# A four-layer decoder trunk on one core: out-projection parts as separate jobs, and two weight splits queued at other places

## The chip, the core and the metric

The kernel runs on one core of a Trainium2 chip. Five engines with queues of their own take part: TensorE (PE in the profile, with its weight loads shown apart as PEld), VectorE (DVE), ScalarE (ACT), GpSimd (POOL) and SyncE (SP), which issues the DMAs. Each engine runs its instructions in the order in which they were queued, and waits on semaphores for what other engines make. The metric is the device time of one launch in microseconds; the number given for a kernel is the median of several runs.

## What is computed

Four layers over 512 tokens of width 1024, in fp32. The mixers are, in turn, latent attention (MLA), sliding-window attention (SWA), forgetting attention (FoX), and MLA again. The part that all layers share:

```
for i in range(DEPTH):                    # 4 layers
    h = x @ w_in                          # q, k, v (or low-rank parts) and a gate
    o = attention(h)                      # 16 heads of 64
    y = (o * silu(gate)) @ w_out          # the out-projection, 1024 x 1024
    x = layernorm(ALPHA * x + y, ln_g[i], ln_b[i])
```

## The kernel before

**Products in split fp32.** Every operand of a product is held as a pair of fp32r tiles, hi (a cast) and lo (the rest), and a product is three matmuls: hi·hi, then the two mixed ones. In the out-projection and in other products with tokens on the output rows the order per contraction slab of 128 is hi·hi, lo·hi (the activation's lo), hi·lo (the weight's lo).

**Weights.** All weights lie in one packed array as units of up to 128x1024 values, in the order of use. `_raw` loads a unit into one of three raw buffers (`wr`) by an SP DMA. `_split(i)` brings all units up to i that are not yet split: ACT casts the raw tile to hi (L306) and POOL, or DVE for out-projection units, subtracts to get lo (L310, two instructions of up to 512 columns). Then the load of the unit two further on is issued. `W(key)` returns a unit and asks for the splits up to three units ahead, though not beyond `self.hold`. A unit of the next layer is not split before `finish` has raised `self.layer`.

**The order of instructions.** The kernel is traced as a program, and a scheduler in the compiler puts each engine's instructions in order by its own estimate of when each is ready. Inside `manual_schedule(engines={PE})` PE keeps the traced order instead, and inside `finish` DVE keeps it too. `run_heads` traces PE's work from the hand-written strings `ORDER[layer]`: each word is a letter and a count of matmuls. s is the next logits matmul, t the next transpose of probabilities, o the next matmul of probabilities and values. f, g and h take the next matmul of the first, second and third job in a list; a job that has come to its count at the front is dropped. The list holds the projections still to be made (gates, queries, keys) and, at its end, the out-projection, which before the change is one job of all its parts in a row: three token blocks of the left half (`half` 0) with contraction slabs 0 to 5, then their slab 6, then the right half and the left half's fourth block with slabs 0 to 6. f, g and h all mean that last job once nothing stands before it.

**The pair outputs.** After the two heads of a pair, ACT and DVE evacuate the result (L543, L544), POOL multiplies by the gate (L551), ACT casts to oT hi (L552) and POOL makes oT lo (L325). Slab p of the out-projection reads oT of pair p. The names A, B, C below are the left-half blocks 0, 1, 2; the number is the slab, and a, b, c are its three matmuls: A5a reads oT hi of pair 5 (heads 10 and 11), A5b reads oT lo, A5c reads hi again.

**The seam of two layers.** `tail` makes the last two heads with what is left of the out-projection (`st["order"]`) in between, and `finish` does the residual and LayerNorm by token block in the order of `FINISH[layer]`: r is the residual (L586), s the mean and squares (L612, ACT L614), t the variance (DVE L619) and 1/std (POOL power, L620), a and b the two halves of the apply (DVE L634, two instructions each, b needs 1/std), x the eight transposes to x^T on PE (L389) with ACT's cast (L393) and DVE's rest (L325). Block 0's x^T is what the next layer's first matmuls read. In the same stretch POOL splits the next layer's first units.

**The start.** Before layer 0, four blocks of x are transposed (`x_transposes`), and the first weight units are loaded and split when the first layer asks for them.

Of the kernel before, what the change touches and what calls it, by code (L numbers as in the profile page):

```python
# [16 lines left out]
ALU = mybir.AluOpType  # L17
# [6 lines left out]
DEPTH = 4  # L24
# [176 lines left out]
class Net:  # L201
# [178 lines left out]
    def x_transposes(self, xt, tb, banks=None):  # L380

        nc = self.nc
        for g in range(2):
            pool, tag = banks or (self.ps_t, "pt")
            ps = pool.tile([128, 512], F32, tag=tag, name=self.nm("pxt"))
            for k in range(4):
                c = (4 * g + k) * 128
                v = ps[:, k * 128:(k + 1) * 128]
                nc.tensor.transpose(v, xt[:, c:c + 128], self.ident[:])  # L389
            src = ps[:].rearrange("p (k n) -> p k n", n=128)  # L390
            hi = self.xT[:, 0, 4 * g:4 * g + 4, tb * 128:(tb + 1) * 128]
            lo = self.xT[:, 1, 4 * g:4 * g + 4, tb * 128:(tb + 1) * 128]
            nc.scalar.copy(hi, src)  # L393
            self.lo(lo, src, hi)

    def xh(self, k):
# [160 lines left out]
    def out_part(self, layer, st):  # L557

        st["acc"] = {}
        st["done"] = 0  # L560
        st["stat"] = self.p_st.tile([128, NT, 4], F32, tag="stat", name=self.nm("stat"))
        self.load_residual(layer, st)
        parts = [(0, tb, range(6)) for tb in range(3)] + [(0, tb, [6]) for tb in range(3)]
        parts += [(half, tb, range(7)) for half, tb in ((1, 0), (1, 1), (1, 2), (0, 3))]
        for half, tb, ks in parts:
            for _ in self.out_mm(layer, st, half, tb, list(ks), False):
                st["done"] += 1 if self.fine else 3
                yield

    def out_mm(self, layer, st, half, tb, ks, stop):  # L570
        if (half, tb) not in st["acc"]:
            if (half, tb) in ((1, 0), (1, 1)):
                st["acc"][(half, tb)] = self.ps_s.tile([128, 512], F32, tag="ss", name=self.nm("po"))
            elif (half, tb) in ((1, 2), (0, 3)):
                st["acc"][(half, tb)] = self.ps_t.tile([128, 512], F32, tag="pt", name=self.nm("po"))
            else:
                st["acc"][(half, tb)] = self.bank()
        out = st["acc"][(half, tb)][:]
        oT = st["oT"]
        return self.tokproj_steps(out, lambda k: (self.W(layer, "O", half, k // 2), (k % 2) * 512), 512,  # L580
                                  lambda k, a, b: oT[k // 2][:, k % 2, a, b * 128:(b + 1) * 128], tb, ks, ks[0] == 0, stop, 3)
# [34 lines left out]
    def ln_rstd(self, st, tb):  # L616
        nc = self.nc
        s = st["stat"][:, tb, 3:4]
        nc.vector.tensor_scalar(s, s, 1.0 / D, LN_EPS, op0=ALU.mult, op1=ALU.add)  # L619
        nc.gpsimd.tensor_tensor(s, s, self.half[:, 0:1], op=ALU.pow)  # L620

    def ln_apply(self, layer, st, tb, part):
        nc = self.nc
# [30 lines left out]
    def run_heads(self, layer, st, make, pre=None, npre=0):  # L654

        kind = layer % 3
        st["P"], st["PT"], st["oT"] = {}, {}, []
        st["np"] = 3 if kind == 0 else 2
        self.heads = 0

        def size(n):
            return {"K": 6, "Q": 9, "R": 9}.get(n, 24) if kind == 0 else 96 if n == "V" else 24

        def logits():
            for h in range(H - 1):
                if h == 13 and kind == 0:
                    self.cq_done(layer)
                for i, f in enumerate(st["s_fn"](h, st)):
                    for j, _ in enumerate(f()):
                        if i == NT - 1 and j == st["np"] - 1:  # L670
                            self.head_done()
                        yield

        jobs = [[npre, pre]] if npre else []
        jobs += [[size(n), make[n](a)] for n, a in STREAM[kind]]
        st["order"] = self.out_part(layer, st)
        jobs.append([1000, st["order"]])
        runs = {"s": logits(), "t": chain.from_iterable(f() for h in range(H - 2) for f in st["t_fn"](h, st)),
                "o": chain.from_iterable(self.attn_pv(h, st) for h in range(H - 2))}
        self.fine = True  # L680
        with self.tc.manual_schedule(engines={mybir.EngineType.PE}):
            for w in ORDER[layer].split():
                for _ in range(int(w[1:])):
                    job = jobs[min("fgh".index(w[0]), len(jobs) - 1)] if w[0] in "fgh" else [0, runs[w[0]]]
                    next(job[1])
                    job[0] -= 1
                    while jobs[0][0] == 0:
                        jobs.pop(0)
            assert len(jobs) == 1 and all(next(r, None) is None for r in runs.values())
            self.tail(layer, st)  # L690

    def tail(self, layer, st):
# [12 lines left out]
    def finish(self, layer, st):  # L705
        nc = self.nc
        self.load_gb(layer, st)
        self.layer = layer + 1
        if layer < DEPTH - 1:
            self.new_xT()  # L710

        def mm(half, tb, ks=(7,)):
            self.run(self.out_mm(layer, st, half, tb, list(ks), True))

        def res(tb, half):
            self.out_res(layer, st, half, tb, st["acc"][(half, tb)][:])

        S0, S1 = lambda tb: self.ln_stats(st, tb), lambda tb: self.ln_rstd(st, tb)
        A = lambda tb, i: self.ln_apply(layer, st, tb, i)

        def X(tb):
            self.x_transposes(st["r"][tb], tb, (self.ps_s, "ss") if tb % 2 == 0 else (self.ps_t, "pt"))

        def ends(tb):
            assert st["done"] >= (84, 105, 126, 147)[tb]
            mm(0, tb)
            if tb < 3:
                mm(1, tb)

        last_mm = self.out_mm(layer, st, 1, 3, list(range(8)), True)  # L730
        todo = {"f": lambda n: self.run(islice(st["order"], n)), "k": ends, "m": lambda n: self.run(islice(last_mm, n)),
                "r": lambda t: (res(t, 0), res(t, 1)), "h": lambda t: res(t, 0), "i": lambda t: res(t, 1), "s": S0, "t": S1,
                "a": lambda t: A(t, 0), "b": lambda t: A(t, 1), "z": lambda t: self.ln_apply_side(st, t), "x": X}
        with self.tc.manual_schedule(engines={mybir.EngineType.DVE}):
            for w in FINISH[layer].split():
                todo[w[0]](int(w[1:]))

    def cq_done(self, layer):
        self.cq_free = layer + 1
# [351 lines left out]
@with_exitstack  # L1091
def trunk(ctx, tc, t):
    net = Net(ctx, tc, t)
    nc = net.nc
    x0 = []
    for tb in range(NT):
        r = net.p_kk.tile([128, D], F32, tag="kk", name=net.nm("x0"))
        for c in range(0, D, 512 if tb == 0 else D):
            w = 512 if tb == 0 else D
            nc.sync.dma_start(r[:, c:c + w], t["x"][tb * 128:(tb + 1) * 128, c:c + w])  # L1100
        x0.append(r)
        if tb < 2:
            net._raw(1 + tb)
    net.new_xT()
    net.warm_up()
    for tb in range(NT):
        net.x_transposes(x0[tb], tb)
    for layer in range(DEPTH):
        (net.mla, net.swa, net.fox)[layer % 3](layer)

# [30 lines left out]
```

## Time and profile before

| what | value |
|---|---|
| runs, median (lowest to highest) | 1026.9 us (1026.78 to 1029.99), 3 runs |
| the profiled execution's own time | 1026.01 us |
| its span in the profile | 1024.2 us |
| instructions | 16213 |
| mean TensorE clock granted | 0.986 of full |
| DVE, ACT, POOL busy | 598.3, 620.8, 510.7 us |
| moved by DMA | 116.79 MB, 114 GB/s |

The profile is of one execution. The span runs from the first to the last instruction; the execution's own time is 1.8 us longer. A row of the timeline gives the start and the length in microseconds, the engine, the source line, the operation, the tile written, the tiles read, the shape and the count of instructions merged in the row; in brackets stands how long the engine was idle before the row, and what ended that idle time. `pp`, `po`, `ss`, `oo`, `ptt` and `pxt` are PSUM tiles (projections, out-projection, logits, head outputs, transposed probabilities, transposed x). In a row of several matmuls, the length is from the first start to the last end, and neighbouring rows can overlap since matmuls are pipelined. In tables by stretch, each engine has its busy time, and PEclk is the clock that TensorE was granted as a share of full.

### The profile page before, as it was taken

To read this page: it belongs to the slowest core of one execution; us is meant where nothing else is said; L and a number is where in the kernel's file an instruction comes from. 1 tells how busy PE (TensorE), PEld (TensorE's weight loads), DVE (VectorE), ACT (ScalarE), POOL (GpSimd) and SP (SyncE) were. 2 spreads that over 40 slices of the span, in tenths; PEclk is the share of its full clock that TensorE was granted. 3 is DMA by queue.
4 is the path that set the end of the run, shared out by engine and by line. 5 is a ranking of instruction groups with operands and counts; after the bars stand their busy time and mean duration, and the time that the engine had idled before them with its cause. 6 is when DMAs were issued, how large, how long until landed. Compare 5 with 4: busy or idle time off the path is not lost.

```text
span 1024.2 us, 16213 instructions
## 1 busy us (share of the span) xinstructions
PE 985.8 (96%) x5512; PEld 856.9 (84%) x5512; DVE 598.3 (58%) x1501; ACT 620.8 (61%) x1354; POOL 510.7 (50%) x572
## 2 busy tenths in 40 slices
PE   8999999999999999899999999997999999999995
PEld 7979888877988888688888888985779888888784
DVE  2467666935546667528325644664547466667827
ACT  4378888843357777523446766663533478888722
POOL 5746655335156663432556666543254647664213
PEclk9999999999999999899999999998999999999998
DMA  6353332634342213223434323353224354334322
GB/s 225 119 157 92 98 106 66 205 111 146 133 143 84 83 63 124 91 94 128 133 120 141 105 88 120 91 144 120 84 84 146 97 145 127 85 94 124 103 62 83
DMA packets 37795, 116.79 MB, mean 114 GB/s; under 512 B 5440, under 2 KB 5696, under 8 KB 37456
## 3 DMA queue, kind: packets, MB, share of 16 engines
q1 hardware_dynamic: 37712, 115.75, 36.5%
q8 instruction: 44, 0.72, 0.3%
q14 instruction: 39, 0.32, 0.1%
HBM read 92.62 MB, written 8.42 MB: 99 GB/s over the span
## 4 chain that ended last, share of the span: by engine, by line
PE 47%; DVE 3%; issue 2%; POOL 1%; ACT 1%; DMA 1%; DVEq 0%; POOLq 0%; SPq 0%; ACTq 0%
PE pp L322 31%; PE ss L322 4%; PE po L322 4%; PE oo L322 3%; PE ptt L514 3%; DMA wr<-in_w 1%; PE pxt L389 1%; POOL r L650 1%; DVE w L310 1%; DVE r L634 0%; POOL P L462 0%; DVE PT L325 0%; ACT P L451 0%; DVE wo L310 0%; DVE r L586 0%
## 5 line engine op out<-in xcount | busy, mean ns | idle before, releaser
L322 PE MATMUL pp<-xT,w 128*128 128x512 f32 (+1 forms) x1440 | 352.4, 387 | 0.0
L310 POOL TENSOR_TENSOR w<-wr,w 128x512 fp32r<-128x512 f32 (+1 forms) x202 | 242.2, 1224 | 193.0 <-ACT w L306 127.2
L322 PEld LDWEIGHTS pp<-xT,w 128*128 128x128 f32 x1440 | 256.1, 188 | 44.2
L462 POOL TENSOR_TENSOR P<-P,rs 128x256 f32<-128x256 f32 (+2 forms) x192 | 113.0, 616 | 136.8 <-DVE rs L457 131.3
L306 ACT CAST w<-wr 128x1024 fp32r<-128x1024 f32 (+5 forms) x121 | 116.1, 964 | 87.4 <-PE pp L322 43.5
L451 ACT ACTIVATE P<-P,m 128x256 f32<-128x256 f32 (+3 forms) x256 | 137.8, 539 | 45.9 <-DVE m L1069 17.0
L325 DVE TENSOR_TENSOR PT<-ptt,PT 128x384 fp32r<-128x384 f32 (+1 forms) x176 | 104.0, 600 | 52.6 <-ACT PT L500 51.3
L500 ACT CAST PT<-ptt 128x384 fp32r<-128x384 f32 (+1 forms) x176 | 88.3, 515 | 47.6 <-PE ptt L514 34.6
L322 PE MATMUL pp<-w,xT 128*128 128x256 f32 (+2 forms) x768 | 112.7, 300 | 2.9 <-ACT xT L393 2.5
L322 PEld LDWEIGHTS pp<-w,xT 128*128 128x128 f32 x768 | 105.8, 191 | 4.6 <-ACT xT L393 3.1
L322 PE MATMUL oo<-PT,v 128*128 128x256 f32 (+3 forms) x512 | 106.6, 313 | 2.3 <-DVE o L544 1.6
L322 PEld LDWEIGHTS oo<-PT,v 128*128 128x128 f32 x512 | 83.5, 189 | 14.0 <-DVE o L544 2.6
L322 PE MATMUL pp<-w,oT 128*128 128x512 f32 x288 | 82.5, 422 | 10.9 <-ACT oT L552 7.5
L322 PE MATMUL ss<-kt,q 128*128 128x128 f32 (+3 forms) x384 | 81.8, 328 | 2.2 <-ACT kt L838 1.6
L322 PE MATMUL pp<-cT,w 128*128 128x512 f32 x312 | 81.6, 397 | 0.0
L885 DVE CUSTOM_DVE_ANT_0 P<-ss,mask 128x128 f32<-128x128 f32 (+3 forms) x128 | 61.1, 484 | 32.4 <-PE ss L322 24.7
L514 PE MATMUL ptt<-ident,P 128*128 128x128 f32 x480 | 78.5, 275 | 1.5 <-DVE PT L325 0.8
L322 PEld LDWEIGHTS pp<-w,oT 128*128 128x128 f32 x288 | 56.0, 202 | 23.4 <-ACT oT L552 8.1
L322 PE MATMUL po<-wo,oT 128*128 128x512 f32 x288 | 71.5, 396 | 0.0
L322 PEld LDWEIGHTS ss<-kt,q 128*128 128x128 f32 x384 | 60.7, 189 | 8.8 <-ACT kt L838 2.2
L514 PEld LDWEIGHTS ptt<-ident,P 128*128 128x128 f32 x480 | 57.1, 140 | 11.8 <-PE ss L322 2.1
L544 DVE TENSOR_TENSOR o<-oo,o 64x512 f32<-64x512 f32 x64 | 43.9, 686 | 37.4 <-ACT o L543 36.7
(120 smaller groups left out, 1425.9 us busy)
## 6 DMA issues: line engine op xcount, KB each, us to landing
wr<-in_w SPq DMA_DIRECT2D x106, 512.0 KB, 3.5
q<-rq SPq DMA_DIRECT2D x64, 128.0 KB, 2.4
xd<-r SPq DMA_DIRECT2D x12, 512.0 KB, 2.9
r<-xd SPq DMA_DIRECT2D x12, 512.0 KB, 3.4
wr<-in_w SPq DMA_DIRECT2D x16, 336.0 KB, 3.4
kd<-kd SPq DMA_DIRECT2D x20, 256.0 KB, 3.2
tq<-in_cs SPq DMA_DIRECT2D x8, 512.0 KB, 4.0
cb<-cd SPq DMA_DIRECT2D x16, 256.0 KB, 3.9
```

Of the source, the lines that this page charges most:

```text
L306: nc.scalar.copy(w[0][:, :c], r[:, :c])
L310: eng.tensor_tensor(w[1][:, a:b], r[:, a:b], w[0][:, a:b].bitcast(F32), op=ALU.subtract)
L322: self.nc.tensor.matmul(out, l, r, start=start, stop=stop)
L325: (eng or self.nc.vector).tensor_tensor(out, src, hi.bitcast(F32), op=ALU.subtract)
L389: nc.tensor.transpose(v, xt[:, c:c + 128], self.ident[:])
L451: nc.scalar.activation(v, v, AF.Exp, bias=m[:, c:c + 1], scale=-1.0, accum_out=sums[:, c:c + 1])
L462: nc.gpsimd.tensor_tensor(v, v, rs[:, c:c + 1].to_broadcast([128, v.shape[1]]), op=ALU.mult)
L500: nc.scalar.copy(pt[:, 0, :n], ps[:, :n])
L514: nc.tensor.transpose(ps[:, c:c + 128], Ps[qb][:, kb * 128:(kb + 1) * 128], self.ident[:])
L544: nc.vector.tensor_tensor(o[a, :], o_ps[a, :], o[a, :], op=ALU.add)
L650: nc.gpsimd.tensor_tensor(v, v, st["gb"][2 * part + c][:], op=op)
L885: nc.vector.tensor_tensor_reduce(out=P[:, :n], in0=ps[:, :n], in1=self.mask[:, S - n:], scale=1.0, scalar=3e38, op0=ALU.add, op1=ALU.min, ...
```

## The change

There are three edits.

1. `out_part` returns a list of ten jobs, one for each part, where it was one generator. f, g and h are no longer cut off at the last job: g and h now reach the second and third part of the out-projection while an earlier part is unfinished. The `ORDER` strings are the same. The tail gets the chain of the jobs that are left.
2. In `finish`, `self.hold` is set so that the calls of `W` split two units of the next layer where they split three. The third is split after the `FINISH` steps have been traced, and inside `issue_after(st["pow"][1])`: its POOL instructions are queued behind block 1's 1/std, with no wait for it to end. ACT's cast of that unit has no such edge.
3. At the start, unit 0 is split inside `issue_after(net.cast)`, traced after block 0's transposes: ACT's cast of it is queued behind ACT's second x^T cast.

What edit 1 does to PE's order follows from the strings. In layer 0 nothing changes. In the others (the count of instructions in brackets):

```
layer 1 before: A0a..A4c  s14(2) A5a s14(2) A5b A5c  B0a..B3c  o12(3) t13(4) o12(5)
                B4a t13(3) B4b B4c B5a B5b B5c  C0a..C0c  o13(8)
layer 1 after:  A0a..A4c  s14(2) B0a s14(2) B0b..B4c  o12(3) t13(4) o12(5)
                A5a t13(3) B5a A5b A5c B5b B5c  C0a..C0c  o13(8)
layer 2 before: A4a..A5c  B0a..B3b o12(1) B3c s14(2) t12(3) o12(3) B4a B4b s14(2) B4c B5a..C0b
                t13(4) C0c C1a s14(2) C1b C1c C2a o12(1) C2b o12(3) C2c s14(2) t13(3) C3 t13(3) o13(8)
layer 2 after:  A4a..A4c  B0a..B4b o12(1) B4c s14(2) t12(3) o12(3) A5a B5a s14(2) C0a..C1c
                t13(4) C2a C2b s14(2) C2c A5b A5c o12(1) B5b o12(3) B5c s14(2) t13(3) C3 t13(3) o13(8)
layer 3 before: A5a A5b A5c B0a B0b o12(1) B0c s14(6) B1a..
layer 3 after:  A5a B0a B0b B0c B1a o12(1) A5b s14(6) A5c B1b..
```

The same matmuls are made in each; what is left for the tail is the same too. The third unit of edit 2 is the first key unit in layer 1 (128x1024), the third value unit in layer 2 (128x544) and the third unit of the low-rank projection in layer 3 (128x672).

```diff
@@ def x_transposes(self, xt, tb, banks=None):
-            nc.scalar.copy(hi, src)
+            self.cast = nc.scalar.copy(hi, src).ins
             self.lo(lo, src, hi)
@@ def out_part(self, layer, st):
         st["stat"] = self.p_st.tile([128, NT, 4], F32, tag="stat", name=self.nm("stat"))
-        self.load_residual(layer, st)
         parts = [(0, tb, range(6)) for tb in range(3)] + [(0, tb, [6]) for tb in range(3)]
         parts += [(half, tb, range(7)) for half, tb in ((1, 0), (1, 1), (1, 2), (0, 3))]
-        for half, tb, ks in parts:
+
+        def part(half, tb, ks):
+            if "r" not in st:
+                self.load_residual(layer, st)
             for _ in self.out_mm(layer, st, half, tb, list(ks), False):
                 st["done"] += 1 if self.fine else 3
                 yield
+
+        return [[3 * len(ks), part(half, tb, ks)] for half, tb, ks in parts]
@@ def ln_rstd(self, st, tb):
-        nc.gpsimd.tensor_tensor(s, s, self.half[:, 0:1], op=ALU.pow)
+        st["pow"][tb] = nc.gpsimd.tensor_tensor(s, s, self.half[:, 0:1], op=ALU.pow).ins
@@ def run_heads(self, layer, st, make, pre=None, npre=0):
-        st["order"] = self.out_part(layer, st)
-        jobs.append([1000, st["order"]])
+        jobs += self.out_part(layer, st)
...
-                    job = jobs[min("fgh".index(w[0]), len(jobs) - 1)] if w[0] in "fgh" else [0, runs[w[0]]]
+                    job = jobs["fgh".index(w[0])] if w[0] in "fgh" else [0, runs[w[0]]]
...
-            assert len(jobs) == 1 and all(next(r, None) is None for r in runs.values())
+            assert all(next(r, None) is None for r in runs.values())
+            st["order"] = chain.from_iterable(g for _, g in jobs)
             self.tail(layer, st)
@@ def finish(self, layer, st):
         self.layer = layer + 1
+        st["pow"] = {}
+        first = self.index[(layer, "O", 1, 3)] + 1
+        self.hold = first + 1
...
                 todo[w[0]](int(w[1:]))
+        self.hold = len(self.units)
+        if layer < DEPTH - 1:
+
+            with self.tc.issue_after(st["pow"][1]):
+                self._split(first + 2)
@@ def trunk(ctx, tc, t):
         net.x_transposes(x0[tb], tb)
+        if tb == 0:
+            with tc.issue_after(net.cast):
+                net._split(0)
```

## The prediction

> **What bounds the kernel now.** I read the page's first part, then the waits of TensorE. PE is busy for nearly the whole span, so time can come only from its idle gaps and from stretches in which it runs slowly.
>
> ```profile
> PE 985.8 (96%) x5512; PEld 856.9 (84%) x5512; DVE 598.3 (58%) x1501; ACT 620.8 (61%) x1354; POOL 510.7 (50%) x572
> ...
> PE pp L322 <- ACT oT L552: 7.5, 2, 3.9
> PE pxt L389 <- DVE r L634: 4.4, 5, 2.0
> PE pp L322 <- POOL oT L325: 3.2, 2, 2.6
> PE pp L322 <- ACT xT L393: 2.5, 1, 2.5
> ```
>
> The columns of a wait are its total, how often, and the longest. Three kinds matter, and each edit aims at one: 10.7 us for oT in front of an out-projection matmul (edit 1), 4.4 us for block 0's apply at the seams (edit 2), 2.5 us at the start (edit 3). The table by stretches of 5 us then says where PE was slow without being idle.
>
> ```profile
> 410.00:415.00 5.00, 1.40 (x6) 1.03 (x5) 4.41 (x8) 2.69 (x5) 2.92 (x4) 0.93 0.56 167
> 415.00:420.00 5.00, 4.87 (x13) 3.70 (x12) 1.00 (x5) 2.67 (x10) 1.56 (x3) 0.50 0.00 0
> ...
> 705.00:710.00 5.00, 2.12 (x4) 1.42 (x5) 0.00 (x0) 0.19 (x1) 3.62 (x4) 0.50 0.01 4
> 710.00:715.00 5.00, 5.00 (x14) 3.86 (x14) 0.00 (x0) 0.00 (x0) 0.00 (x0) 0.53 0.00 0
> ...
> 765.00:770.00 5.00, 4.64 (x17) 3.79 (x18) 5.00 (x8) 2.52 (x4) 5.00 (x5) 0.66 0.73 213
> ```
>
> The third column from the right is the granted clock. It drops to half behind the two oT stalls, and to 0.66 behind the longest seam wait. So a stall costs its idle time and some microseconds at half speed behind it. Meanwhile the other engines and the DMA have almost nothing to do: removing these stretches takes time from nobody.
>
> The Trainium skill, "TensorE: Matmul & The Clock Gate", Part 1, says that about 3.4 us without PE activity halve the clock, and the same time of activity restores it; the oT stalls of 3.6 us and more agree.
>
> **Edit 1, layer 1.** PE's timeline:
>
> ```profile
> 407.69 2.88 PE L322 MATMUL pp<-w,oT 128*128 128x512 f32 x12
> 410.42 0.40 PE L322 MATMUL ss<-kd,q 128*128 128x256 f32 x2
> 414.41 0.80 PE L322 MATMUL pp<-w,oT 128*128 128x512 f32 x1 [3.60 <-ACT oT L552]
> ...
> 415.76 5.96 PE L322 MATMUL pp<-w,oT 128*128 128x512 f32 x14
> 421.55 0.52 PE L322 MATMUL oo<-PT,v 128*128 128x256 f32 x3
> ...
> 413.74 0.62 ACT L552 CAST oT<-o 128x512 fp32r<-128x512 f32 x1 [0.20 <-POOL o L551]
> 414.43 1.27 POOL L325 TENSOR_TENSOR oT<-o,oT 128x512 fp32r<-128x512 f32 x1 [0.73 <-ACT oT L552]
> ```
>
> A5a waits for oT hi of pair 5, written at 414.36, and A5b for lo at 415.70. From 410.82 to 421.55, 10.7 us, PE makes 15 matmuls of 512 columns and two logits. At full clock twelve such matmuls take 410.42 - 407.69 = 2.73 us, 0.2275 each; 15 take 3.4, and the two logits 0.4. After the change the 15 are B0a to B4c, whose pairs 0 to 4 A has read already. So o12 comes at 414.6 and not 421.55: **7.0 us**. Its inputs allow that:
>
> ```profile
> 412.38 1.16 DVE L325 TENSOR_TENSOR PT<-ptt,PT 128x512 fp32r<-128x512 f32 x2
> 414.04 0.42 DVE L947 CUSTOM_DVE_ANT_0 P<-ss,ali 128x256 f32<-128x256 f32 x1
> ...
> 415.67 0.42 DVE L947 CUSTOM_DVE_ANT_0 P<-ss,ali 128x256 f32<-128x256 f32 x1 [1.20 <-PE ss L322]
> ...
> 419.14 1.54 POOL L462 TENSOR_TENSOR P<-P,rs 128x128 f32<-128x128 f32 x3 [3.44 <-DVE rs L457]
> ...
> 426.73 0.60 PE L969 MATMUL ptt<-ident,P 128*128 128x128 f32 x4
> ```
>
> Head 12's transposed probabilities are there at 413.54. A5a now stands behind o12's eight matmuls and seven of head 13's small ones, near 416, with both halves of oT written. What is late next is head 14: its transposes start 426.73 - 421.55 = 5.2 us after o12, so at 419.8 in the new order. Its last logits are reduced at 415.67 now; then that instruction follows the one of 414.04, at 414.5. From there to POOL's last product took 415.67 to 420.68, 5.0 us, so 419.5, or up to 421.3 if ACT's three evacuations of heads 12 and 13 (0.6 each, as the cast at 413.74) fall among its exponentials. A new wait of 0 to 1.5; I take 0.6. Net **-6.4**.
>
> **Edit 1, layer 2.**
>
> ```profile
> 700.40 0.95 PE L322 MATMUL pp<-w,oT 128*128 128x512 f32 x3
> 705.24 0.80 PE L322 MATMUL pp<-w,oT 128*128 128x512 f32 x1 [3.90 <-ACT oT L552]
> 708.67 5.91 PE L322 MATMUL pp<-w,oT 128*128 128x512 f32 x13 [2.63 <-POOL oT L325]
> 714.39 0.53 PE L322 MATMUL oo<-PT,v 128*128 128x512 f32 x1
> ...
> 704.59 0.60 ACT L552 CAST oT<-o 128x512 fp32r<-128x512 f32 x1
> ...
> 703.15 0.69 DVE L325 TENSOR_TENSOR PT<-ptt,PT 128x512 fp32r<-128x512 f32 x1
> ...
> 707.36 1.26 POOL L325 TENSOR_TENSOR oT<-o,oT 128x512 fp32r<-128x512 f32 x1
> ```
>
> A4c ends its turn at 700.40 + 3 x 0.2275 = 701.1. Before, o12 follows at 714.39 with 14 matmuls in between; after, 14 of B take 3.2 us and o12 comes at 704.3, its probabilities written at 703.84: **10.1 us**. A5a then stands ten short instructions behind (about 706; oT hi is there at 705.19), and A5b some nineteen further (about 709.5; lo is there at 708.62). Both margins are under 1 us, so I take 0.2 of new waits, 0 to 1.3. Net **-9.9**.
>
> **Layer 3**: no wait stands at A5a there, so the shuffle costs and gives nothing; layer 0 is the same. The residual's DMAs on SP stay at the first out-projection matmul.
>
> **Edit 2.** The DVE and POOL rows around block 0's and 1's apply at the first seam, and PE's:
>
> ```profile
> 249.75 3.12 POOL L310 TENSOR_TENSOR w<-wr,w 128x512 fp32r<-128x512 f32 x2 [0.79 <-ACT w L306]
> 249.97 3.45 DVE L634 SCALAR_TENSOR_TENSOR r<-r,stat,ln_b 128x512 f32<-128x512 f32 x2
> 256.23 1.71 POOL L620 TENSOR_TENSOR stat<-stat,half 128x1 f32<-128x1 f32 x2 [3.35 <-DVE stat L619]
> 257.97 1.41 DVE L634 SCALAR_TENSOR_TENSOR r<-r,stat,ln_b 128x512 f32<-128x512 f32 x2 [0.44 <-POOL stat L620]
> 258.93 1.17 PE L389 MATMUL pxt<-ident,r 128*128 128x128 f32 x8
> ...
> 260.42 1.84 PE L322 MATMUL pp<-xT,w 128*128 128x256 f32 x14
> ...
> 765.09 0.66 PE L389 MATMUL pxt<-ident,r 128*128 128x128 f32 x4 [2.03 <-DVE r L634]
> ...
> L634 DVE SCALAR_TENSOR_TENSOR r<-r,stat,ln_b x28: 737/744/1793, 250.0 to 1015.9; 128x512 f32<-128x512 f32 x28
> ```
>
> Block 0's apply takes 3.45 us beside a POOL split and 1.41 alone; its largest single duration is 1793 ns against a median of 744. That stretching, not the 1/std, makes PE wait. But the POOL split beside it is not the third unit: it is a later one, which has no edge behind the power and may run there again. The third unit comes behind block 1's 1/std, at 257.9, exactly beside block 1's apply at 257.97. There PE stands ready for it at 258.93: two instructions stretched by up to 1.05 each cost up to 2.1, and I take **+1.7** for this seam. At the second, residuals from PSUM lie between the 1/std and block 1's apply, and at the third PE has other work, so 0 there. The bounds: all seam waits gone, 4.4, with the clock loss of 765 to 770, 0.34 x 5 = 1.7, so -6.1; or 2.1 at each seam, +6.3. The unit's ACT cast and its load two units on (SP) are traced behind `finish` with it, and one of three raw buffers stays taken for that long; the later units that this holds up are read later still. The unit itself is in time: its lo, written by 261.0 (257.9 and 3.1 as at 249.75), is first read by the seventeenth key matmul, and these start at 260.42 with 0.13 each, so at 262.5.
>
> **Edit 3.**
>
> ```profile
> 6.64 0.75 ACT L306 CAST w<-wr 128x672 fp32r<-128x672 f32 x1 [4.63 <-DMA wr<-in_w]
> 7.47 1.76 POOL L310 TENSOR_TENSOR w<-wr,w 128x512 fp32r<-128x512 f32 x2 [6.17 <-ACT w L306]
> 7.93 0.51 PE L322 MATMUL pp<-w,xT 128*128 128x336 f32 x1 [2.55 <-ACT xT L393]
> ```
>
> The x^T casts now sit behind a weight cast that waits for its DMA. In the other order they are done earlier, and the first matmul starts when the weight cast ends, 7.39 and not 7.93: up to 0.5. The third matmul needs POOL's lo, which doesn't move. I take **-0.3** of 0 to 0.5.
>
> **Sum.** -6.4 - 9.9 + 1.7 - 0.3 = -14.9 on an execution of 1026.0, so 1011.1. The median of the runs lies 0.9 above that execution: 1012.0.
>
> **Rivals.**
> - *The seams gain* (14%). The scheduler leaves POOL free beside block 0's apply: -6.1 in place of +1.7, 1004. For it: one unit less stands on POOL there. Against it: the next unit is loaded and free to slip in.
> - *The third unit stretches block 1's apply at all seams* (18%): +6.3, 1016.6. The Trainium skill, "GPSIMD Engine Reference", section 8, says that GpSimd shares its SBUF interfaces with VectorE and contends with its instructions of two SBUF inputs; the 3.45 beside 1.41 agrees. By it the edit only moves the contention.
> - *Vector engines take back the lead* (13%). PE now comes 7 and 10 us early to head 14, whose chain through DVE, ACT and POOL is no shorter. It decides from about 2 us, where the wait at 765 brought 1.7 of clock loss too: twice 3.7, less the 0.8 counted, 1018.6. For it: in layer 1 the chain's margin is used up. Against it: in layer 2 all other engines stood still behind the stall.
> - *The change doesn't do what it says* (4%): A5 is moved, but oT of pair 5 is queued later on ACT and POOL, which the scheduler orders anew, and the stalls stand again: 1026.
> - *Slower* (3%). The scheduler orders ACT, DVE and POOL anew in layers 1 to 3. One op misplaced on POOL in front of a pair output makes a stall like those above, 7.0 us with its half clock. It decides from the third new stall (two give back the gain): 3 x 7.0 = 21, 1033. Against it: layers 0 and 3 run the same scheme without one.
>
> **How the numbers follow.** My own case has 48%, 1009 to 1014. A measurement can tell about 0.3%, 3 us, from no change. Faster: all but the last two cases, 0.93; same 0.04; slower 0.03. The range runs from the seam gain to the vector engines' case and holds the rest but a few per cent and the tails of each: 1004 to 1019.
>
> **What would show it.** The oT waits of L552 gone from PE's list, granted clock 1.00 in the stretches that follow, o12 about 4.2 us behind A4c in layer 1 and 3.2 in layer 2; at the first seam, block 1's apply near 3 us. Wrong would be: half clock in the tails of layers 1 and 2, a new wait of over 2 us for P or PT, or block 0's apply at 1.4 us.

## The result, and the profile after

| kernel | median (lowest to highest) | ratio to before, 95% interval |
|---|---|---|
| before | 1026.84 us (1026.27 to 1029.99), 4 runs | |
| changed | 1017.72 us (1016.75 to 1019.60), 4 runs | 0.9907 (0.9882 to 0.9932) |

The change gains 9.1 us where 14.9 were forecast. Both stalls for oT are gone, as forecast; 2.3 of the gain is given back at once in layer 1, and the seams of the layers became slower, not faster. The page's first part for the changed kernel, profiled in an execution of 1016.75 us:

```profile
span 1015.0 us, 16214 instructions
...
PE 983.1 (97%) x5512; PEld 856.2 (84%) x5512; DVE 601.7 (59%) x1501; ACT 620.5 (61%) x1354; POOL 513.7 (51%) x572
```

TensorE's waits in it (total, how often, longest). The waits for oT behind L552 are not among them. In their place, and in place of the 2.5 us for xT at the start, stand others:

```profile
PE pxt L389 <- DVE r L638: 4.6, 4, 1.5
PE oo L322 <- DVE o L544: 3.0, 4, 1.6
PE pp L322 <- ACT P L781: 1.7, 1, 1.7
...
PE pxt L389 <- DMA x<-in_x: 0.9, 1, 0.9
```

Edit 2 was aimed at the wait for r, the output of the apply (L634 before, L638 now): it is 4.6 us in all, and it was 4.4. The table by stretches has the granted clock in the third column from the right:

```profile
410.00:415.00 5.00, 5.00 (x25) 4.19 (x25) 4.94 (x8) 3.49 (x7) 3.65 (x4) 1.00 0.48 135
415.00:420.00 5.00, 4.73 (x29) 3.81 (x27) 2.61 (x10) 3.34 (x13) 1.48 (x2) 1.00 0.12 44
470.00:475.00 5.00, 2.34 (x16) 1.77 (x15) 4.14 (x8) 2.74 (x7) 4.01 (x4) 0.97 0.77 234
475.00:480.00 5.00, 5.00 (x31) 5.00 (x32) 5.00 (x10) 1.17 (x2) 0.99 (x1) 0.69 0.48 191
700.00:705.00 5.00, 5.00 (x27) 4.23 (x26) 4.17 (x12) 4.13 (x9) 2.02 (x3) 1.00 0.85 290
705.00:710.00 5.00, 5.00 (x29) 4.33 (x28) 2.47 (x10) 2.06 (x6) 3.50 (x4) 1.00 0.01 2
```

The tails of layers 1 and 2 (410 to 420, 700 to 710) now run at full clock, and without a gap but for 0.3 us before 420, where a new wait begins. But at 470 to 480, the second seam, TensorE is busy for less than half of a stretch and then gets 0.69: that is new.

**The two traces side by side.** TensorE makes the same 5512 matmuls in both kernels. So the start of the n-th matmul in one trace, less that of the n-th in the other, is how far the one is behind, and where this difference changes, time was lost or won. (Where two kernels order a stretch differently, it is read behind the stretch.) Worked out that way, in us against the profiled execution of before:

| stretch | forecast | changed kernel | the same again, e7 |
|---|---|---|---|
| start, up to matmul 600 | -0.3 | +1.1 | +1.1 |
| layer 0, up to its tail's end | 0 | 0.0 | +1.1 |
| first seam | +1.7 | +0.3 | +1.7 |
| layer 1's tail | -6.4 | -4.9 | -4.9 |
| second seam | 0 | +3.2 | +3.5 |
| layer 2's tail | -9.9 | -10.2 | -10.1 |
| third seam | 0 | +1.3 | +1.3 |
| layer 3 | 0 | -0.2 | +1.9 |

**Layer 1's tail.** The timeline of TensorE, VectorE, GpSimd and ScalarE there, in the changed kernel:

```profile
412.58 3.36 PE L322 MATMUL pp<-w,oT 128*128 128x512 f32 x14
...
415.78 0.52 PE L322 MATMUL oo<-PT,v 128*128 128x256 f32 x3
...
415.86 0.42 DVE L959 CUSTOM_DVE_ANT_0 P<-ss,ali 128x256 f32<-128x256 f32 x1
...
415.93 1.29 POOL L325 TENSOR_TENSOR oT<-o,oT 128x512 fp32r<-128x512 f32 x1 [0.73 <-ACT oT L552]
...
416.32 0.92 DVE L449 TENSOR_SCALAR m<-m,nsink 128x4 f32<-128x4 f32 x1
...
417.28 0.40 ACT L451 ACTIVATE P<-P,m 128x128 f32<-128x128 f32 x1 [1.42 <-DVE m L449]
...
419.93 0.58 ACT L543 COPY o<-oo 64x512 f32<-64x512 f32 x1
...
420.55 0.68 DVE L544 TENSOR_TENSOR o<-oo,o 64x512 f32<-64x512 f32 x1
...
421.28 0.61 PE L322 MATMUL oo<-PT,v 128*128 128x256 f32 x3 [1.55 <-DVE o L544]
```

The 14 matmuls take 3.36 us where they took 5.96, and o12 starts at 415.78, 7.2 us ahead on the side-by-side count. Then o13 waits 1.55 for the one PSUM tile of the head outputs, which ACT and DVE empty from 419.93 to 421.23, behind head 14's exponentials on ACT (from 417.28). Counted up to the end of o13's eight matmuls, which have a short gap of their own, 2.3 come back.

**First seam.** POOL, DVE and PE around the apply of blocks 0 and 1:

```profile
248.40 0.56 POOL L624 TENSOR_TENSOR stat<-stat,half 128x1 f32<-128x1 f32 x1 [14.75 <-DVE stat L623]
...
251.14 1.41 DVE L638 SCALAR_TENSOR_TENSOR r<-r,stat,ln_b 128x512 f32<-128x512 f32 x2
...
257.59 9.32 POOL L310 TENSOR_TENSOR w<-wr,w 128x512 fp32r<-128x512 f32 x6
...
257.66 3.44 DVE L638 SCALAR_TENSOR_TENSOR r<-r,stat,ln_b 128x512 f32<-128x512 f32 x2 [0.44 <-POOL stat L624]
...
259.48 0.66 PE L389 MATMUL pxt<-ident,r 128*128 128x128 f32 x4 [0.89 <-DVE r L638]
261.16 0.66 PE L389 MATMUL pxt<-ident,r 128*128 128x128 f32 x4 [1.02 <-DVE r L638]
```

POOL stands idle for 14.75 us ahead of block 0's 1/std. Block 0's apply is at 1.41, and block 1's takes 3.44, as block 0's did before (3.45). Behind block 1's power come not one unit's lo halves but three units': x6, the third and the two that follow it.

**Second seam**, the same engines:

```profile
457.44 1.11 POOL L624 TENSOR_TENSOR stat<-stat,half 128x1 f32<-128x1 f32 x1 [13.59 <-DVE stat L623]
...
458.72 1.41 DVE L638 SCALAR_TENSOR_TENSOR r<-r,stat,ln_b 128x512 f32<-128x512 f32 x2
...
462.72 10.80 POOL L310 TENSOR_TENSOR w<-wr,w 128x512 fp32r<-128x512 f32 x8
...
464.45 3.29 DVE L638 SCALAR_TENSOR_TENSOR r<-r,stat,ln_b 128x512 f32<-128x512 f32 x2
...
469.18 3.21 DVE L638 SCALAR_TENSOR_TENSOR r<-r,stat,P 128x512 f32<-128x512 f32 x2 [0.46 <-ACT jk L618]
...
474.87 1.97 PE L389 MATMUL pxt<-ident,r 128*128 128x128 f32 x8 [1.50 <-DVE r L638]
```

Here four units, the third and three more (x8), run in a block of 10.80 us behind block 1's power. Beside them block 1's apply takes 3.29 where it took 1.40, and the first half of block 2's takes 3.21 where it took 1.42; block 2's own power has its place behind them on POOL (473.48). PE waits 1.50 and makes its next eight transposes in 1.97, at half clock; block 0's eight, at 460.24, took 1.03.

**Third seam.** Rows of DVE, ACT and PE:

```profile
753.05 1.42 DVE L638 SCALAR_TENSOR_TENSOR r<-r,stat,ln_b 128x512 f32<-128x512 f32 x2 [0.32 <-POOL stat L624]
...
763.02 0.76 ACT L306 CAST wo<-wr 128x672 fp32r<-128x672 f32 x1 [1.72 <-DMA wr<-in_w]
...
768.28 6.54 PE L322 MATMUL pp<-w,xT 128*128 128x336 f32 x31 [1.72 <-ACT P L781]
```

Here edit 2 first wins what it was meant to win: block 0's apply takes 1.42 (2.68 before), PE's wait for it falls from 2.03 to 1.18, no half clock follows, and PE is 2.6 us better off. Then it loses 3.9. The block of splits frees a raw buffer so late that the load for the cast at 763.02 is issued at 759.72 only (in e1 below, which has the old order there, at 755.21). Behind that cast stand, in ACT's queue, the squares of block 2's LayerNorm, behind these, on DVE, block 2's apply and a copy of the projection, and behind the copy ACT's P. PE waits 1.72 for it, with half clock from 768.24 on.

### The profile page after: what moved, and what is told of

The parts are those of the page before. It is cut to its first block, busy times and chain, and to the rows that moved or that the text cites. A ratio compares the mean times of both kernels' runs of the same rounds, so it can differ in the third digit from the quotient of the medians.

```text
span 1015.0 us, 16214 instructions
## 1 busy us (share of the span) xinstructions
PE 983.1 (97%) x5512; PEld 856.2 (84%) x5512; DVE 601.7 (59%) x1501; ACT 620.5 (61%) x1354; POOL 513.7 (51%) x572
## 4 chain that ended last, share of the span: by engine, by line
PE 79%; DVE 6%; ACT 4%; issue 4%; POOL 4%; DMA 3%; SPq 0%; DVEq 0%; POOLq 0%; ACTq 0%
PE pp L322 51%; PE ss L322 8%; PE po L322 7%; PE oo L322 6%; PE ptt L514 5%; POOL w L310 2%; DMA wr<-in_w 2%; PE pxt L389 1%; ACT P L451 1%; PE ptt L981 1%; DVE PT L325 1%; POOL r L654 1%; DMA x<-in_x 1%; DVE wo L310 1%; DVE r L638 1%
## 5 line engine op out<-in xcount | busy, mean ns | idle before, releaser
L322 PE MATMUL pp<-w,xT 128*128 128x256 f32 (+2 forms) x768 | 116.4, 305 | 4.3 <-ACT P L781 1.7
L322 PEld LDWEIGHTS pp<-w,xT 128*128 128x128 f32 x768 | 109.0, 195 | 6.3 <-ACT P L781 2.3
L322 PE MATMUL pp<-w,oT 128*128 128x512 f32 x288 | 76.1, 397 | 0.6 <-POOL oT L325 0.6
L322 PEld LDWEIGHTS pp<-cT,w 128*128 128x128 f32 x312 | 56.6, 188 | 10.3
```

The source lines that it names most:

```text
L322: self.nc.tensor.matmul(out, l, r, start=start, stop=stop)
```

## The experiments

The theory after these traces (A): edit 1 made all of the gain, edit 2 costs 4.8 us and edit 3 costs 1.1. The rival (B): TensorE now comes 6 and 16 us early to the seams, the vector engines can't follow there, and the losses are edit 1's own. The first three runs make one edit each.

**e1, edit 1 alone**: `out_part` and `run_heads` of the change, everything else as before.

> Edit 1 alone (the out-projection's parts as own jobs). Theory A, from the two traces laid side by side matmul by matmul: all of the gain belongs to this edit (7.2 + 10.2 us in the tails of layers 1 and 2, 2.3 given back in layer 1), and the other two edits cost 4.8 us at the seams and 1.1 at the start. So 1026.8 - 15.1 = 1011.7 us, ratio 0.985, with block 0's apply stretched to near 3.45 us at the first seam as before. Theory B, the vector engines take back the lead: TensorE comes 6 and 16 us early to the second and third seam and the others can't follow there. Then about 1017 us, ratio 0.991, and new waits at those seams without edit 2.

Measured: 1014.53 us, 0.9871 (0.9842 to 0.9899). The stretches: layer 1's tail -4.9, layer 2's tail -10.2, all three seams 0.0. So the losses at the seams are not edit 1's, and B falls. The whole time is 2.8 us over A's number, and the profiled execution shows where: +1.6 at the start and +3.0 in layer 0, where not one instruction stands elsewhere than before (the last section comes back to it). A's 0.985 lies in the interval.

**e2, edit 2 alone**: `hold`, the edge and the later split.

> Edit 2 alone (the third weight unit behind block 1's 1/std). Theory A: +0.3, +3.2 and +1.3 us at the three seams, 4.8 together: 1031.6 us, ratio 1.005, with GpSimd idle for 13 to 15 us ahead of block 0's 1/std at the first two seams, block 0's apply at 1.41 us and block 1's near 3.3 us. Theory B: 0 or a small gain, 1024 to 1027 us, ratio 0.997 to 1.000. The recorded forecast for this part: +1.7, ratio 1.0017.

Measured: 1032.59 us, 1.0056 (1.0037 to 1.0074). The seams: +1.7, +3.2, +1.3. Its second seam has the changed kernel's rows, without edit 1:

```profile
464.65 1.11 POOL L620 TENSOR_TENSOR stat<-stat,half 128x1 f32<-128x1 f32 x1 [13.59 <-DVE stat L619]
...
469.93 10.79 POOL L310 TENSOR_TENSOR w<-wr,w 128x512 fp32r<-128x512 f32 x8
...
482.08 1.97 PE L389 MATMUL pxt<-ident,r 128*128 128x128 f32 x8 [1.50 <-DVE r L634]
```

The same 13.59 of idle POOL, the same block of eight, the same wait of 1.50. The edit costs 5.8 us by the ratio (0.0056 x 1027), at least 3.8 by its interval, and the recorded +1.7 (1.0017) is outside. A stands for this edit.

**e3, edit 3 alone.**

> Edit 3 alone (first weight cast behind the first x^T casts). Theory A: +1.1 us, ratio 1.001, all of it within the first 20 us: the first matmul comes 0.7 earlier, then TensorE takes block 1's transposes, whose x is not there. Theory B and the recorded forecast: -0.3 us or nothing.

Measured: 1026.39 us, 1.0001 (0.9983 to 1.0019): no difference. Its profiled execution is 1.5 us behind after 600 matmuls, but so is e1's (1.6), which has the old start. Matmul 60 comes 0, 1.6, 1.1, -0.7, 1.6 and 0.6 us late in the six profiled executions with the old order, and 0.9, 0.9, 1.3, 0.0 and -0.2 late in the five with the new one. The +1.1 that A gave this edit was one execution's luck: A falls here. The edit does what it says: the first projection matmul starts at 7.21 in the changed kernel and 7.63 here, where it started at 7.93 before. But the x of block 1 is there only at 9.1, and PE waits 0.94 and 0.88 for it. What is left is nothing that shows; a gain of 0.3 would be too small to be seen in these runs.

**e4, the changed kernel without the edge**: which part of edit 2 empties POOL?

```diff
-            with self.tc.issue_after(st["pow"][1]):
-                self._split(first + 2)
+            self._split(first + 2)
```

> The changed kernel, with the third unit still traced behind the seam but with no edge behind block 1's 1/std. It tells the edge from the place in the program. If the edge is what empties GpSimd ahead of block 0's 1/std, the splits run there again and the seams stand as before the change: 1017.7 - 4.8 = 1012.9 us, ratio 0.986. If the later place in the program alone puts the whole run of splits behind the seam, it stays at 1017 to 1018 us, ratio 0.991, with the same idle GpSimd.

Measured: 1014.96 us, 0.9880 (0.9854 to 0.9905). The seams: -0.1, 0.0, +0.2. POOL is back at splits from 241.9 and 450.8 us, ahead of block 0's power, and block 0's apply stands at 3.46 again. So it is the edge; `hold` and the later place in the program do nothing alone. Nor do the later units wait for data: at the changed kernel's second seam the load of the fifth unit had landed by 447.51 and ACT stood idle from 450.61 to 455.93, but ACT's casts of the fourth and fifth come at 461.83 and 462.78 (here at 451.39 and 452.75). The scheduler gave them a later place in the queues. The whole time is 2 us over the number expected, whose 0.986 lies in the interval.

**e5, the third unit alone moved.** The recorded forecast took the edit to move one unit. Here it does: the two that follow are split ahead of it, with no edge (`_one` is the body of `_split` for one unit).

```diff
-            with self.tc.issue_after(st["pow"][1]):
-                self._split(first + 2)
+            self._raw(first + 4)
+            self._one(first + 3)
+            self._one(first + 4)
+            with self.tc.issue_after(st["pow"][1]):
+                self._one(first + 2)
+            self.split_done = first + 5
+            self._raw(first + 6)
```

> The changed kernel, with the two units that follow the third split ahead of it and with no edge, so that the third alone waits for block 1's 1/std: this is what the recorded forecast took the edit for. Theory A' (the loss comes from the whole run of later splits queued behind the third): GpSimd makes four lo halves ahead of block 0's 1/std at the first two seams, block 2's apply stands alone again at 1.4 us, and of the 4.8 us lost at the seams the second seam's 3.2 goes to 1 or less; with edits 1 and 3 about 1012 us + 1.5, ratio 0.985 to 0.988. Rival (the third unit alone, beside block 1's apply, is the loss): the seams stay at +4 to +5, 1017 us, ratio 0.991.

Measured: 1012.22 us, 0.9851 (0.9826 to 0.9877). The seams: +0.2, -0.6, -0.1; together -0.5 against +4.8. The second seam of this kernel (lines are shifted: L316 is the split, L628 the power, L642 the apply):

```profile
451.71 5.04 POOL L316 TENSOR_TENSOR w<-wr,w 128x512 fp32r<-128x512 f32 x4 [7.25 <-ACT w L312]
...
458.06 1.11 POOL L628 TENSOR_TENSOR stat<-stat,half 128x1 f32<-128x1 f32 x1 [1.30 <-DVE stat L627]
...
459.34 1.41 DVE L642 SCALAR_TENSOR_TENSOR r<-r,stat,ln_b 128x512 f32<-128x512 f32 x2
...
463.33 4.45 POOL L316 TENSOR_TENSOR w<-wr,w 128x512 fp32r<-128x512 f32 x4
...
465.07 3.26 DVE L642 SCALAR_TENSOR_TENSOR r<-r,stat,ln_b 128x512 f32<-128x512 f32 x2
...
469.76 1.41 DVE L642 SCALAR_TENSOR_TENSOR r<-r,stat,P 128x512 f32<-128x512 f32 x2 [0.46 <-ACT jk L622]
```

The fourth and fifth unit run in the empty time before the power, and the block behind block 1's power is two units (x4, the third and the sixth) where it was four. Block 2's apply stands alone again. Block 1's is still stretched, to 3.26, and PE has other work there. So the loss is the run of units behind the third, not the third beside block 1's apply.

**e6, edit 1 with head 14's last logits earlier.** The new wait of 1.55 in layer 1: is it the queue of head 14's softmax? One string of PE's order changes:

```diff
-... f1 s2 f19 s2 g1 s2 g14 o3 t4 o5 f1 t3 g1 f7 o8
+... f1 s2 f7 s2 g1 s2 f12 g14 o3 t4 o5 f1 t3 g1 f7 o8
```

> Edit 1 alone, with head 14's last two rows of logits made 12 matmuls (2.7 us) earlier in layer 1's tail. In edit 1 alone VectorE reduces them at 418.66, behind two lo halves, an output's sum, two PT halves and a gate, and ScalarE makes the four exponentials at 420.42, ahead of PT of head 13 and of head 12's output, for which TensorE waits 1.57. Theory (this queue is the new wait): the reductions come near 416.3, the exponentials are done by 419.5, the 1.57 falls under 0.3, and up to 0.8 of it comes back as waits for the output's lo, made a us later: -0.5 to -1.5 us against edit 1 alone in that tail. Rival (TensorE simply runs ahead of everything there): the wait comes back whole at another tile, 0.

Measured: 1010.17 us, 0.9830 (0.9805 to 0.9855). Layer 1's tail: -5.7 where edit 1 alone has -4.9. The exponentials and the wait:

```profile
415.33 0.22 DVE L449 TENSOR_SCALAR m<-m,nsink 128x4 f32<-128x4 f32 x1
...
415.59 0.40 ACT L451 ACTIVATE P<-P,m 128x128 f32<-128x128 f32 x1 [0.27 <-DVE m L449]
...
419.61 0.62 PE L322 MATMUL oo<-PT,v 128*128 128x256 f32 x3 [0.76 <-DVE o L544]
```

The wait halves, from 1.57 to 0.76. In edit 1 alone the first exponential comes 1.5 us behind o12 (418.90 to 420.42), here 0.7 (414.89 to 415.59). It is not under 0.3 as expected: the reductions moved ahead in DVE's order, but the small instruction on m that follows them (415.33) stayed behind two PT halves and a gate, and starts 0.44 behind o12 where it started 0.57 behind (419.47). The rest of the 0.8 is its length: 0.22 here, 0.92 in edit 1 alone, where it runs beside GpSimd's oT lo (419.08 to 420.36). Here it starts 0.07 ahead of that instruction (415.40), which is luck. So the chain to the exponentials is the wait, and half of it is shown; that its delay is DVE's queue, as the theory had it, is not. The whole run is also lower than e1's, though the intervals overlap. In the profiled executions, 4.8 apart, 0.8 is the string's, and the rest the start (-0.6 against +1.6) and layer 0 (+1.2 against +3.0), where the two kernels are the same.

**e7, the changed kernel again**, beside e5 and e6.

> The changed kernel once more, on the same chip as the two beside it, to set edit 1 alone and the others against it: 1017.7 us as before, ratio 0.991. It also tells what of the first 20 us belongs to the order and what to the execution: if the start is the edit's, its first 60 matmuls end near +0.9 us against the profiled execution of before again; if it is chance, anywhere between 0 and +1.6, as in the executions so far.

Measured: 1018.99 us, 0.9912 (0.9888 to 0.9935). Its interval lies above e6's and e5's as a whole, with the same runs of before: edit 1 with the earlier logits beats the changed kernel, and so does e5.

**e8, the colliding unit to VectorE.** In the old order one unit's split runs beside block 0's apply (two units' at the third seam). Here the lo halves of one unit come from DVE, right behind block 1's apply; the base is e6.

```diff
-            eng = nc.vector if self.units[k][0][1] in DVE_LO else nc.gpsimd
+            eng = nc.vector if self.units[k][0][1] in DVE_LO or k == self.dve else nc.gpsimd
...
+        def U(n):
+            k = self.index[(layer, "O", 1, 3)] + 1 + n
+            self._split(k - 1)
+            self.dve = k
+            self._split(k)
```

The `FINISH` strings get `u4`, `u5` and `u4` behind `b1`.

> Edit 1 and the earlier logits of the run before, and the one unit whose lo halves GpSimd made beside block 0's apply (the fifth of the new layer at the first and third seam, the sixth at the second) gets its lo halves from VectorE, right behind block 1's apply. No edge is added, and the other units stay where they were. Theory (the stretching is contention of VectorE's apply with the GpSimd split beside it): block 0's apply at 1.41 us at all three seams, block 1's at 1.41 too, TensorE's waits for r go from 4.4 to under 1 us and the half clock behind the third seam goes: -3 to -6 us against that run, ratio 0.977 to 0.980. Rival (the wait moves to whatever VectorE now does later, since the two added operations of 0.6 each stand in its queue ahead of blocks 2 and 3): 0 to +3 us.

Measured: 1016.01 us, 0.9906 (0.9890 to 0.9923): slower than its base. In the profiled executions 2.1 of the loss is the start, where the two are the same, and 3.0 the first seam (+2.9 against -0.1):

```profile
252.15 1.41 DVE L638 SCALAR_TENSOR_TENSOR r<-r,stat,ln_b 128x512 f32<-128x512 f32 x2
...
258.60 2.96 POOL L310 TENSOR_TENSOR w<-wr,w 128x512 fp32r<-128x512 f32 x2
258.66 3.44 DVE L638 SCALAR_TENSOR_TENSOR r<-r,stat,ln_b 128x512 f32<-128x512 f32 x2 [0.44 <-POOL stat L624]
...
262.02 1.28 DVE L310 TENSOR_TENSOR w<-wr,w 128x512 fp32r<-128x512 f32 x2
...
263.97 3.52 PE L322 MATMUL pp<-xT,w 128*128 128x256 f32 x16 [1.04 <-DVE r L590]
```

Block 0's apply is at 1.41 at the first two seams, as the theory of contention has it; at the third it is still 2.57, beside the fourth and sixth unit's splits, where the fifth and sixth had run in e6. But at the first seam the expectation had named the wrong unit: by the order of the casts the sixth ran beside block 0's apply, and the fifth, which the edit gives to VectorE, had run in POOL's empty time. The sixth now runs behind block 1's power (258.60). There it stretched block 1's apply to 3.44, and the split on DVE stood ahead of a residual (L590) for which PE then waited 1.04. The rival was right about VectorE's queue, and with one collision taken away there was another. (The second seam gained 0.4.)

**e9, TensorE kept busy in a wait.** Ten transposes of the identity, which nobody reads, ahead of block 0's transposes at the third seam; the base is e6.

```diff
+            if layer == 2 and tb == 0:
+                ps = self.ps_o.tile([128, 512], F32, tag="oo", name=self.nm("fill"))
+                for i in range(10):
+                    nc.tensor.transpose(ps[:, i % 4 * 128:i % 4 * 128 + 128], self.ident[:], self.ident[:])
```

> Edit 1 with the earlier logits, and ten transposes of the identity, read by nobody, that TensorE makes at the third seam while it waits 2.17 us for block 0's apply. All six executions so far in which that wait stood whole show half clock for 3.4 us behind it. Theory (the clock falls where TensorE runs for less than about half of a 3.41 us window, and a transpose counts as running): the ten fill about 1 us of the wait, the window's share goes from 0.38 to 0.6 or more, the granted clock stays 1.00 at 748 to 756, and the matmuls behind come 1.5 us earlier. Rival (the wait for the apply itself, or the lack of ordinary matmuls, lowers the clock): half clock there as before, 0. The scheduler orders some of layer 3's first instructions anew with the ten in, which may hide the gain in the whole time: 1008 to 1011 us, ratio 0.981 to 0.984.

Measured: 1013.26 us, 0.9854 (0.9822 to 0.9886), which tells nothing of 1.5 us. The stretch itself does. First e6, then e9:

```profile
750.00:755.00 5.00, 4.72 (x18) 3.71 (x19) 5.00 (x7) 2.58 (x4) 5.00 (x6) 0.66 0.74 219
```

```profile
750.00:755.00 5.00, 3.74 (x26) 2.97 (x25) 4.68 (x6) 3.53 (x6) 5.00 (x5) 1.00 0.39 90
```

The clock stays at 1.00, from here to the program's end, where e6 has half clock from 751.45 to 754.86. PE waits 0.99 behind the ten. That this is not the luck of the grid on which the clock changes (last section) can be worked out: the window of 3.413 us here begins at 750.77, and matmuls run in 0.63 of it; without the ten it would be 0.31, and every window that low in these traces was followed by half clock. The third seam is 1.5 us shorter than before (counted behind it, with ten matmuls allowed for; e6 has +0.2). Some of layer 3's first instructions come in another order in e9, so that the 1.5 is not the clock's alone beyond doubt; the clock itself is shown.

## Why the forecast was half right

- **Both oT stalls: right.** o12 comes 7.2 us earlier in layer 1 (7.0 forecast) and layer 2's tail is 10.2 shorter (10.1 forecast, 9.9 net). The clock stays full behind them. The new waits at A5a and A5b, 0.2 in layer 2, did not come. The sentence that the other engines have almost nothing to do in the slow stretches was read too widely: it holds for layer 2's rows (DVE 0.00 at 705 to 715), not for layer 1's (DVE 4.41 of 5.00 at 410 to 415), and it is in layer 1 that a part came back.
- **The new wait in layer 1: mis-sized, and at another place.** 2.3 came back where 0.6 was taken, outside the 0 to 1.5 allowed. The working was right that head 14's logits are reduced about when o12 starts (414.5 and 414.6 forecast, 415.86 and 415.78 measured). It looked for the wait at head 14's transposes, with ACT's evacuations delaying the exponentials. The exponentials went first, and later than counted: the small instruction on m took 0.92 (at 416.32), beside GpSimd's oT lo (415.93 to 417.22), where it took 0.23 before (at 416.13). It takes 0.23 in all 78 cases of the eleven traces in which GpSimd does nothing beside it. So the evacuations were late, and o13 waited for its PSUM tile. e6, in which the first exponential comes 0.8 earlier, halves the wait.
- **Edit 2: the step that failed** is the sentence that a later unit "has no edge behind the power and may run there again". The units that follow went behind the third and with it, three in all at the first seam (x6) and four at the second (x8). Block 1's apply near 3 us was right (3.44), but what had been named as the sign of being wrong, block 0's apply at 1.4, appeared as well. The first seam was +0.3 and +1.7 in the two executions (forecast +1.7), the second only with half clock behind it: PE's waits of 0.20 and 1.02 for block 0 went, and 0.89 and 1.02 for block 1 came, a trade that the forecast had not counted as one. The second and third seam, put at 0, cost 3.2 to 3.5 and 1.3, the third by the raw buffers held longer, which the forecast named and gave no price. e4 shows that the edge does it, e5 that without the queue behind it the same edge costs nothing. Why the compiler's scheduler leaves POOL idle rather than pass the third unit is not shown.
- **The rivals.** The third unit beside block 1's apply at all seams, +6.3, is nearest in size (+4.8 to +6.5), but through several units, and where it cost most it was block 2's apply and power beside and behind them. The apply pair takes 1.41 us alone against 3.2 to 3.46 beside a split at the first two seams. The Trainium skill, "GPSIMD Engine Reference", section 8, has GpSimd share its SBUF interfaces with VectorE; these rows agree. The vector engines' taking back the lead, which the forecast saw at head 14, came in part in layer 1 (the 2.3) and not in layer 2; the like of it at the seams, B, fell with e1.
- **Edit 3: nothing that shows** (-0.3 forecast). The first matmul does start earlier, but then waits for x. The first 20 us vary by 2.3 us from execution to execution with the order unchanged, which the 0 to 0.5 of the forecast had not seen, since it stood on one execution.

The sum: -15.1 from edit 1, +4.8 from edit 2, +1.1 at the start, -0.1 elsewhere, -9.3 in the profiled execution. That 1017.7 lies in the range of 1004 to 1019 is in part luck: its slow end came from the vector engines' case, 3.7 us given back in each of two tails. Of that 2.3 came, in one tail; the rest of the shortfall came from edit 2, whose effect on POOL's queue the forecast did not see.

## What to carry to other kernels

An edge on one instruction holds back whatever the scheduler queues behind it, so look at each engine's whole queue after it, above all for an engine that falls idle in front. Where one engine comes earlier, ask of each producer what stands in its queue ahead of the result, not only when its input is there. And a stretch in which two kernels run the same instructions shows what chance is worth: here up to 3 us, more than edit 3 and most single seams.

## What the runs showed of the hardware

**The clock falls by window.** In each of the eleven profiled executions all half-clock stretches start on one grid of 3.413 us, whose phase is not tied to the program's start. Worked out from the matmul rows (their ends are modelled), with a window's share being the part of it in which a matmul or transpose ran: of 3187 windows at full clock, all 38 with a share under 0.496 were followed by half clock, 4 of 9 from 0.496 to 0.562, and none of the 3140 above. So a wait of about 2 us may cost 1.5 more, or nothing, as it falls on the grid: the first seam's two waits for r (0.89 and 1.02) cost +0.3 in the changed kernel's first profile and +1.7 in its second, where half clock stood from 263.05 to 266.47. The Trainium skill, "TensorE: Matmul & The Clock Gate", Part 1, has the free-running window of 3413 ns. It speaks of an idle window; here half an idle one is enough, so the forecast's sentence on 3.4 us without activity asked for too much. In e9 the ten transposes counted as activity.

**When a weight's load is issued moves the end by 3 us.** In layer 0's tail before and e1 have the same order on every engine. The casts of two weight units and the wait that follows, first before, then e1:

```profile
201.51 1.05 ACT L306 CAST wo<-wr 128x1024 fp32r<-128x1024 f32 x1 [0.87 <-DMA wr<-in_w]
...
207.16 1.20 PE L322 MATMUL oo<-PT,v 128*128 128x512 f32 x5 [0.38 <-DVE o L544]
```

```profile
204.23 1.05 ACT L306 CAST wo<-wr 128x1024 fp32r<-128x1024 f32 x1 [2.71 <-DMA wr<-in_w]
...
207.41 1.05 ACT L306 CAST w<-wr 128x1024 fp32r<-128x1024 f32 x1 [1.04 <-DMA wr<-in_w]
...
210.55 1.21 PE L322 MATMUL oo<-PT,v 128*128 128x512 f32 x5 [2.17 <-DVE o L544]
```

ACT stands at a cast whose weight lands later, with a head's output behind it in its queue, and TensorE waits 2.17 instead of 0.38, with 3.4 us of half clock behind that. Over all profiled executions this stretch varies from 0.0 to +3.3 us.

The load that is late for the first cast takes as long as before, 3.14 and 3.15 us; it is issued late, at 201.06 where it was 198.35, 1.1 later when the 1.6 of the start are taken off. It waits for a raw buffer that VectorE reads until 200.98, because the last lo half of another unit, beside GpSimd's oT lo (from 198.78), takes 1.78 where its first half took 0.69. Before, oT lo came later, since ACT had waited for a load that took 5.9 us (4.2 in e1), and it met a half whose buffer nobody was waiting for. So a late landing won time here: that load took 5.9 and 6.4 us in the two executions with 0.0, and 4.2 to 4.7 in the nine with +0.7 to +3.3.
